# A planned order for the two token halves around each norm, a fourth column behind it, and the layer norm's first mean added in PSUM

## The chip, the cores and the metric

The kernel runs on one core of a Trainium2 chip. Its work is done by TensorE (matrix products, PE in the profile; PEld are its weight loads), VectorE (DVE), ScalarE (ACT) and GpSimd (POOL), and SyncE's queue (SP) starts the transfers. The metric is the device time of one execution in microseconds (us).

## The reference, cut to what matters

The input is a sequence of 512 tokens with 1024 features. A first block of two layers (attention, then a gated spatial unit, each followed by a convolutional feed-forward network) uses RMS norms; a second block of two layers (a recurrent unit, then dilated attention, with two SwiGLU networks each) uses layer norms around scaled residual sums. All is in float32. Around a norm this is computed:

```python
def rms_norm(x, g):
    y = x * rsqrt(mean(x * x, axis=-1, keepdims=True) + EPS)
    return y * g

def layer_norm(x, g, b):
    mu = mean(x, axis=-1, keepdims=True)
    xc = x - mu
    var = mean(xc * xc, axis=-1, keepdims=True)
    return xc * rsqrt(var + LN_EPS) * g + b

x = x + g2 * conv_ffn(modulate(rms_norm(x, ffn_norm[l]), sh2, sc2), ...)
x = layer_norm(DEEPNORM_ALPHA * x + swiglu(x, w_in, w_out), g, b)
```

## The kernel before, in words

Features lie on the partitions: the residual x is eight tiles x0 to x7 of 128 features by 512 tokens. Every product of a weight and an activation is done as three passes of a reduced float32 type, high times high, high times low and low times high (`mm`, lines 190 to 192). A weight chunk (128 output features, up to eight input tiles) is loaded by SyncE's queue and split by `chunk`: ScalarE makes the high part `wh` (line 145), VectorE the low part `wl` (line 148). Three raw and seven split chunks have buffers at a time. Of PSUM's eight banks six (`b1`) serve the products, two (`norm`) the norms.

A stage ends with `out_gemm`: eight output column tiles of 128 features, each a sum over the hidden tiles. `update` adds a finished bank to its x tile (line 468 or 507), ScalarE squares the tile (315), VectorE adds the square to `acc` (316). The last four column tiles (three after the recurrent unit, six before the last norm) are *held*: they are done first for tokens 0 to 255 (half 0), then for 256 to 511 (half 1). So the norm of half 0 can be worked out while TensorE does the held tiles of half 1.

The norm of a half is: column sums of `acc` by TensorE (281); a chain of small VectorE instructions on 128x2 (lines 270 to 274, three Newton steps for the inverse root); a *spread* of the result to rows (copy 287, transposes 291); then eight *rows*, one for each x tile. A row of an RMS norm is one VectorE instruction and a split (ScalarE high, VectorE low). A row of a layer norm is two VectorE instructions (545, 546), the high part (552) and a float32 copy (553) by ScalarE, and the low part by GpSimd (554).

A layer norm also keeps the sum of x in `accs`, by GpSimd (521). To keep the variance exact, the mean over the first 256 features is taken off all tiles as soon as x0 and x1 are done: their sum (510) times a matrix of ones on TensorE (512), scaled by ScalarE (513), is subtracted from x0 to x4 by VectorE and from x5 to x7 by GpSimd (515).

Behind the norm the next stage's `Head` starts its first columns by halves: three columns of a feed-forward network, of the recurrent unit's input, of the keys or of the queries; the spatial unit has its own head over token tiles. Head step k needs row k of the norm. The order within each engine is chosen by the framework's scheduler from its own estimates, from the order of the code and the dependences.

There are ten such norms: four RMS norms (after the first attention, the first convolutional network, the spatial unit and the second network), then six layer norms (after the first SwiGLU network, the recurrent unit, the second network, the third, the second attention and the last network). The last has no head.

## Time and profile before

| what | value |
|---|---|
| median of three runs | 3490.24 us (3489.15 to 3495.66) |
| the profiled execution, and its span | 3490.69 us, 3488.9 us |
| TensorE busy | 3318.5 us, 95% |
| VectorE, ScalarE, GpSimd busy | 59%, 40%, 11% |
| chain that ended last | TensorE 82%, VectorE 10%, ScalarE 3% |
| mean granted clock of TensorE | 0.979 of full speed |

A busy TensorE is one that has an instruction in it; matrix products overlap, so the time of one is read from start to start. The granted clock is 1.00 at the higher of TensorE's two levels and 0.5 at the lower.

### The profile page before, as it was taken

How to read it: one execution, taken by the hardware profiler on the slowest of the kernel's cores; microseconds unless marked ns; L12 is line 12 of the kernel's file. 1: busy time of each engine (PE TensorE's matmuls, PEld its weight loads, DVE VectorE, ACT ScalarE, POOL GpSimd, SP SyncE). 2: the span in 40 equal slices, each digit the busy share in tenths (PEclk: the TensorE clock that was granted, in tenths of full speed). 3: DMA queues.
4: the chain of work that ended last, by engine and by line, in shares of the span. 5: the costliest groups of instructions: out<-in, count | busy, mean ns of one | idle time of the engine just before them, and what ended most of it. 6: DMA issues, size and time to landing. Idle time of an engine off the chain costs nothing.

```text
span 3488.9 us, 43165 instructions
## 1 busy us (share of the span) xinstructions
PE 3318.5 (95%) x16662; PEld 2823.7 (81%) x16662; DVE 2056.9 (59%) x3419; ACT 1403.9 (40%) x2129; POOL 366.9 (11%) x375
## 2 busy tenths in 40 slices
PE   4888899999999999999999999999999899989998
PEld 3777788888888888888888888889888888788887
DVE  8777887865574555333776533363333689873335
ACT  4245643334343333222485422242222466652223
POOL 5043000000000000000313100030000322230001
PEclk9888999999999999999999999999999999999999
DMA  5641355643222322223132323235223133133231
GB/s 187 188 153 43 139 178 196 223 140 102 85 91 97 97 91 91 97 85 104 62 108 77 109 97 97 91 129 186 97 91 98 47 100 101 48 107 105 92 100 46
DMA packets 126207, 381.70 MB, mean 109 GB/s; under 512 B 13745, under 2 KB 28209, under 8 KB 125874
## 3 DMA queue, kind: packets, MB, share of 16 engines
q1 hardware_dynamic: 125858, 378.82, 33.4%
q8 instruction: 131, 2.15, 0.3%
q14 instruction: 74, 0.61, 0.1%
q10 hardware_dynamic: 144, 0.13, 0.0%
HBM read 360.54 MB, written 18.35 MB: 109 GB/s over the span
## 4 chain that ended last, share of the span: by engine, by line
PE 82%; DVE 10%; ACT 3%; issue 2%; DMA 2%; POOL 0%; SPq 0%; DVEq 0%; ACTq 0%; POOLq 0%
PE b L191 24%; PE b L192 24%; PE b L190 24%; PE bo L838 1%; PE side L190 1%; PE side L191 1%; PE side L192 1%; PE b L822 1%; DVE wl L148 1%; DVE x L515 1%; DVE nm L806 1%; DVE ptl L148 1%; DVE acc L316 1%; PE s L730 1%; DVE reg L148 1%
## 5 line engine op out<-in xcount | busy, mean ns | idle before, releaser
L191 PE MATMUL b<-reg,wh 128*128 128x512 f32 (+1 forms) x4289 | 1573.6, 369 | 24.4 <-DVE reg L337 14.9
L190 PE MATMUL b<-reg,wh 128*128 128x512 f32 (+1 forms) x4289 | 1543.3, 369 | 35.8 <-ACT reg L336 12.4
L192 PE MATMUL b<-reg,wl 128*128 128x512 f32 (+1 forms) x4289 | 1568.8, 368 | 2.5 <-DVE wl L148 2.4
L145 ACT ACTIVATE wh<-raw 128x1024 fp32r<-128x1024 f32 (+3 forms) x550 | 561.1, 1026 | 1325.6 <-PE b L191 1170.0
L148 DVE TENSOR_TENSOR wl<-raw,wh 128x1024 fp32r<-128x1024 f32 (+3 forms) x550 | 656.6, 1200 | 563.1 <-ACT wh L145 551.5
L191 PEld LDWEIGHTS b<-reg,wh 128*128 128x128 f32 x4289 | 821.7, 192 | 160.5 <-DVE reg L337 17.5
L190 PEld LDWEIGHTS b<-reg,wh 128*128 128x128 f32 x4289 | 803.3, 191 | 173.8 <-ACT reg L336 14.6
L192 PEld LDWEIGHTS b<-reg,wl 128*128 128x128 f32 x4289 | 820.8, 191 | 134.1 <-DVE wl L148 3.9
L515 POOL TENSOR_TENSOR x<-x,shift 128x512 f32<-128x512 f32 x18 | 30.9, 1741 | 2475.7 <-ACT shift L513 2475.7
L592 DVE TENSOR_TENSOR sg<-sg,b 128x512 f32<-128x512 f32 x88 | 60.5, 688 | 281.9 <-PE b L192 281.2
L1535 DVE SCALAR_TENSOR_TENSOR x<-b,x 128x512 f32<-128x512 f32 x64 | 44.3, 692 | 190.1 <-PE b L192 190.1
L315 ACT ACTIVATE sq<-x 128x256 f32<-128x256 f32 (+1 forms) x111 | 52.6, 474 | 176.8 <-DVE x L507 84.7
L145 ACT ACTIVATE reg<-sg 128x512 fp32r<-128x512 f32 x132 | 83.3, 631 | 79.5 <-DVE sg L597 77.4
L371 DVE CUSTOM_DVE_ANT_0 ada<-ada,silu_c,cols 128x1024 f32<-128x1024 f32 x80 | 99.5, 1281 | 14.4 <-DMA ada<-ada 14.2
L145 ACT ACTIVATE pth<-b 128x384 fp32r<-128x384 f32 (+1 forms) x160 | 82.1, 534 | 63.0 <-PE b L822 60.1
L148 DVE TENSOR_TENSOR ptl<-b,pth 128x384 fp32r<-128x384 f32 (+1 forms) x160 | 94.6, 603 | 19.2 <-ACT pth L145 18.1
L148 DVE TENSOR_TENSOR reg<-sg,reg 128x512 fp32r<-128x512 f32 x132 | 90.6, 686 | 22.3 <-ACT reg L145 22.3
L190 PE MATMUL side<-reg,wh 128*128 128x512 f32 x221 | 98.6, 446 | 4.8 <-DVE hn L651 2.8
L822 PE MATMUL b<-ident,e 128*128 128x128 f32 x544 | 84.1, 283 | 15.0 <-DVE ptl L148 7.8
L822 PEld LDWEIGHTS b<-ident,e 128*128 128x128 f32 x544 | 66.0, 145 | 30.6 <-DVE ptl L148 9.0
L191 PE MATMUL side<-reg,wh 128*128 128x512 f32 x221 | 90.0, 407 | 0.4 <-DVE reg L148 0.4
L192 PE MATMUL side<-reg,wl 128*128 128x512 f32 x221 | 90.0, 407 | 0.0
(331 smaller groups left out, 3586.8 us busy)
## 6 DMA issues: line engine op xcount, KB each, us to landing
raw<-up SPq DMA_DIRECT2D x264, 512.0 KB, 3.3
ada<-ada SPq DMA_DIRECT2D x96, 512.0 KB, 4.6
raw<-down SPq DMA_DIRECT2D x96, 448.0 KB, 3.2
raw<-down SPq DMA_DIRECT2D x48, 512.0 KB, 3.3
raw<-q SPq DMA_DIRECT2D x24, 512.0 KB, 3.5
raw<-rg_in SPq DMA_DIRECT2D x20, 512.0 KB, 3.3
raw<-attn_in SPq DMA_DIRECT2D x14, 512.0 KB, 7.0
raw<-rg_out SPq DMA_DIRECT2D x16, 320.0 KB, 2.9
```

The source lines that it names most:

```text
L145: return self.nc.scalar.activation(out=hi, in_=src, func=AF.Copy, scale=scale)
L148: return self.nc.vector.tensor_tensor(out=lo, in0=src, in1=hi.bitcast(F32), op=ALU.subtract)
L190: mm(out=ps, lhsT=ah, rhs=bh, start=first, stop=False)
L191: mm(out=ps, lhsT=ah, rhs=bl, start=False, stop=False)
L192: mm(out=ps, lhsT=al, rhs=bh, start=False, stop=last)
L315: nc.scalar.activation(out=s, in_=src, func=AF.Square)
L316: nc.vector.tensor_tensor(out=acc, in0=acc, in1=s, op=ALU.add)
L371: self.nc.vector.tensor_tensor_reduce(out=r, in0=r, in1=self.silu_c, scale=1.0, scalar=self.col("ada_b", 48 * l + m), op0=ALU.mult, op1=AL ...
L515: (nc.vector if k < 5 else nc.gpsimd).tensor_tensor(out=self.x[k], in0=self.x[k], in1=self.shift, op=ALU.subtract)
L592: nc.vector.tensor_tensor(out=sg, in0=sg, in1=bu, op=ALU.mult)
L822: nc.tensor.transpose(out=b[:, i * P:(i + 1) * P], in_=e[:, (k0 + i) * P:(k0 + i + 1) * P], identity=self.ident)
L1535: self.nc.vector.scalar_tensor_tensor(out=x[m], in0=b, scalar=c, in1=x[m], op0=ALU.mult, op1=ALU.add)
```

## The change

It has four parts.

- `turn`, a planner: after the held tiles of half 0 it lists the held products of half 1, the updates, the norm chains of both halves, their rows and the head steps with an engine, a rank and a duration written by hand, and emits them in the order in which they would start; TensorE, VectorE, ScalarE and GpSimd then keep the order in which the code is written. Only TensorE and VectorE have a time line in the plan.
- Seven heads (five feed-forward networks, the recurrent unit's input, the keys) start four columns instead of three. The fourth weight chunk is split inside the turn (`more`), since its buffer is that of a held tile.
- A layer norm's first mean is no longer subtracted from x2 to x7. TensorE adds it to the bank of each of those column tiles, with one pass (`shift_pass`) of a constant matrix on the sum of x0 and x1. x0 and x1 get it by VectorE from a bank.
- A square and its sum are issued apart, and a head step does its passes with the high part of the activation for all columns before those with the low part.

```diff
 class Head:
     def begin(self):
-        self.w = [self.net.chunk(*a) for a in self.args]
+        self.w = [self.net.chunk(*a) for a in self.args[:3]]
+        self.out = []
+    def more(self):
+        self.w += [self.net.chunk(*a) for a in self.args[3:]]
...
 class ColumnHead(Head):
+    step = property(lambda self: 0.36 * len(self.args))
...
+            for b, w in zip(self.out, self.w):
+                mm(out=b[:, sl], lhsT=w[0][:, k, :], rhs=h, start=k == 0, stop=False)
+                mm(out=b[:, sl], lhsT=w[1][:, k, :], rhs=h, start=False, stop=False)
+            for b, w in zip(self.out, self.w):
+                mm(out=b[:, sl], lhsT=w[0][:, k, :], rhs=l, start=False, stop=k == KD - 1)
+            yield
...
 def out_gemm(...):
-        for n, sl in enumerate(HALVES):
-            for m, ws in held:
-                b = self.bank()[:, 0:256]
-                one(b, ws, sl)
-                updates()
-                done_banks.append((m, b, sl))
-            updates()
-            if head is not None:
-                if n == 0:
-                    head.begin()
-                else:
-                    head.half(HALVES[0])
-            finish(sl)
+        for m, ws in held:
+            b = self.bank()[:, 0:256]
+            one(m, b, ws, HALVES[0])
+            updates()
+            done_banks.append((m, b, HALVES[0]))
+        updates()
+        head = self.head
         if head is not None:
-            head.half(HALVES[1])
+            head.begin()
+        with self.tc.manual_schedule(engines=FULL_ORDER):
+            self.turn(held, ..., xs, update, [finish(sl) for sl in HALVES], head, shifted)
...
+    def turn(self, held, ks, xs, update, fin, head, shifted):
+        rows_dur = 0.87 if shifted else 0.9
+        chain_dur = 3.7 if shifted else 2.9
+        free = item("wait", 0, 0.0, None)
+        items[free][5] = 1.9
+        sums = [free, None]
...
+                prev = item("PE", 5, 0.36, lambda ...: product(bank, ws, n), () if prev is None else (prev,))
+            x = item("DVE", 0, 0.45, lambda ...: late.append(update(m, bank[0], sl)), (prev,), 0.15)
+            sums[1] = item("DVE", 1, 0.62, lambda late=late: late[0](), (x,), 0.6)
+        more = None if head is None else item("DVE", 3, 1.25, head.more, (free,), 1.3)
+        for n, gen in enumerate(fin):
+            c = item("PE", 1, 0.5 if shifted else 0.25, go(gen), (sums[n],), 0.25 if n else 0.0)
+            c = item("DVE", 2, chain_dur, go(gen), (c,), 0.2)
+            c = item("PE", 0, 0.45 if shifted else 0.25, go(gen), (c,), 0.2)
+            for k in range(KD + 1):
+                c = item("DVE", 4, rows_dur if k < KD else 0.45, go(gen), (c,), 0.0 if k else 0.25)
+                rows.append(c)
+        if head is not None:
+            for n in range(2):
+                gen = head.half(HALVES[n])
+                for k in range(KD):
+                    r = (KD + 1) * n + k
+                    prev = item("PE", 5, head.step, go(gen), (prev,))
+                    items[prev][4] += [(rows[r], 0.7), (rows[r + 1], -rows_dur + 0.02), (more, 0.02)]
...
+                    t = max([at[engine]] + [items[n][5] + lag for n, lag in needs])
+                    if best is None or (t, rank, i) < best[:3]:
...
+        for _, _, f in sorted(plan, key=lambda z: z[:2]):
+            f()
...
+    def shift_pass(self, ps, sl):
+        self.nc.tensor.matmul(out=ps, lhsT=self.mean, rhs=self.shift[:, sl], start=False, stop=True)
...
 def ln_update(self, m, ps, scale, sl):
         if m == 1:
-            s = self.tmp()
-            nc.vector.tensor_tensor(out=s, in0=self.x[0], in1=self.x[1], op=ALU.add)
+            self.mean = self.means[scale]
+            nc.vector.tensor_tensor(out=self.shift, in0=self.x[0], in1=self.x[1], op=ALU.add)
             b = self.bank()
-            nc.tensor.matmul(out=b, lhsT=self.ones, rhs=s, start=True, stop=True)
-            nc.scalar.activation(out=self.shift, in_=b, func=AF.Copy, scale=1.0 / 256)
-            for k in range(KD):
-                (nc.vector if k < 5 else nc.gpsimd).tensor_tensor(out=self.x[k], in0=self.x[k], in1=self.shift, op=ALU.subtract)
+            nc.tensor.matmul(out=b, lhsT=self.mean, rhs=self.shift, start=True, stop=True)
+            for k in range(2):
+                nc.vector.scalar_tensor_tensor(out=self.x[k], in0=b, scalar=scale, in1=self.x[k], op0=ALU.mult, op1=ALU.add)
...
-        return ColumnHead(self, [("up", 44 * i + m, 8) for m in (0, FF, 1)])
+        return ColumnHead(self, [("up", 44 * i + m, 8) for m in FFN_HEAD])
```

What this does to the order of instructions is shown at three places of the first layer norm (after the first SwiGLU network, the fifth of the ten). The first is VectorE while TensorE does the held products of half 1. Before, update 6, the spread's copy, the sums and update 7 come ahead of the first rows (lines 545, 546; `x6` is the x tile, `norm` the spread rows, `sq` a square):

```order
L538 SCALAR_TENSOR_TENSOR ln_y_2487_13489<-ln_s_2488_13490,ln_y_2487_13489 128x2
L507 SCALAR_TENSOR_TENSOR x6_868_3636<-b1_2519_13627,x6_868_3636 128x256
L287 COPY spread_2490_13507<-ln_y_2487_13489 128x512
L316 TENSOR_TENSOR acc_2136_11271<-acc_2136_11271,sq_2522_13677 128x256
L507 SCALAR_TENSOR_TENSOR x7_869_3637<-b1_2521_13654,x7_869_3637 128x256
L545 TENSOR_TENSOR tmp_2508_13530<-x0_862_3630,norm_2491_13509 128x256
L546 TENSOR_TENSOR tmp_2508_13530<-tmp_2508_13530,norm_2491_13509 128x256
L545 TENSOR_TENSOR tmp_2509_13536<-x1_863_3631,norm_2491_13509 128x256
L316 TENSOR_TENSOR acc_2136_11271<-acc_2136_11271,sq_2523_13682 128x256
L546 TENSOR_TENSOR tmp_2509_13536<-tmp_2509_13536,norm_2491_13509 128x256
```

In the changed kernel (651 is the update, 574 the sum, 692 and 693 a row), from the spread's copy on:

```order
L375 COPY spread_2492_13618<-ln_y_2489_13600 128x512
L651 SCALAR_TENSOR_TENSOR x4_866_3634<-b1_2485_13570,x4_866_3634 128x256
L651 SCALAR_TENSOR_TENSOR x5_867_3635<-b1_2493_13620,x5_867_3635 128x256
L163 TENSOR_TENSOR wl_2500_13675<-raw_2498_13672,wh_2499_13674 128x1024
L651 SCALAR_TENSOR_TENSOR x6_868_3636<-b1_2494_13643,x6_868_3636 128x256
L574 TENSOR_TENSOR acc_2142_11390<-acc_2142_11390,sq_2495_13655 128x256
L574 TENSOR_TENSOR acc_2142_11390<-acc_2142_11390,sq_2497_13667 128x256
L574 TENSOR_TENSOR acc_2142_11390<-acc_2142_11390,sq_2502_13691 128x256
L692 TENSOR_TENSOR tmp_2519_13731<-x0_862_3630,norm_2496_13660 128x256
L693 TENSOR_TENSOR tmp_2519_13731<-tmp_2519_13731,norm_2496_13660 128x256
L651 SCALAR_TENSOR_TENSOR x7_869_3637<-b1_2501_13685,x7_869_3637 128x256
```

The low part of the fourth weight chunk (`wl`) now stands between updates 5 and 6, and three sums come behind it, ahead of the first row.

The second place is VectorE at the second chain, that of half 1 (`ln_s`, `ln_v`, `ln_m2`, `ln_y` and `rsq_b` are its 128x2 values). Before, rows of half 0 stand between its instructions:

```order
L546 TENSOR_TENSOR tmp_2511_13548<-tmp_2511_13548,norm_2491_13509 128x256
L545 TENSOR_TENSOR tmp_2512_13554<-x4_866_3634,norm_2491_13509 128x256
L535 TENSOR_TENSOR ln_m2_2529_13767<-ln_s_2531_13769 128x2
L546 TENSOR_TENSOR tmp_2512_13554<-tmp_2512_13554,norm_2491_13509 128x256
L545 TENSOR_TENSOR tmp_2513_13560<-x5_867_3635,norm_2491_13509 128x256
L536 SCALAR_TENSOR_TENSOR ln_v_2528_13766<-ln_m2_2529_13767,ln_v_2528_13766 128x2
L546 TENSOR_TENSOR tmp_2513_13560<-tmp_2513_13560,norm_2491_13509 128x256
L545 TENSOR_TENSOR tmp_2514_13566<-x6_868_3636,norm_2491_13509 128x256
L270 TENSOR_SCALAR ln_y_2530_13768<-ln_v_2528_13766 128x2
L546 TENSOR_TENSOR tmp_2514_13566<-tmp_2514_13566,norm_2491_13509 128x256
L545 TENSOR_TENSOR tmp_2515_13572<-x7_869_3637,norm_2491_13509 128x256
```

In the changed kernel it begins behind row 4 and runs on to its spread's copy without a row between:

```order
L692 TENSOR_TENSOR tmp_2529_13793<-x4_866_3634,norm_2496_13660 128x256
L693 TENSOR_TENSOR tmp_2529_13793<-tmp_2529_13793,norm_2496_13660 128x256
L677 COPY ln_s_2533_13814<-norm_2528_13788 128x2
L678 TENSOR_SCALAR ln_v_2530_13811<-norm_2528_13788 128x2
L679 TENSOR_TENSOR ln_m2_2531_13812<-ln_s_2533_13814 128x2
L680 SCALAR_TENSOR_TENSOR ln_v_2530_13811<-ln_m2_2531_13812,ln_v_2530_13811 128x2
L359 TENSOR_SCALAR ln_y_2532_13813<-ln_v_2530_13811 128x2
L361 TENSOR_TENSOR rsq_b_2534_13819<-ln_y_2532_13813 128x2
L362 SCALAR_TENSOR_TENSOR rsq_b_2534_13819<-rsq_b_2534_13819,ln_v_2530_13811 128x2
L363 SCALAR_TENSOR_TENSOR ln_y_2532_13813<-rsq_b_2534_13819,ln_y_2532_13813 128x2
L361 TENSOR_TENSOR rsq_b_2534_13819<-ln_y_2532_13813 128x2
```

Row 5, which before stood between the chain's instructions, now comes behind the whole chain.

The third place is TensorE at the head's start (`ident`, `spread`: the transposes; `ones`: column sums; `reg0_0` the high part of row 0, `reg0_8` its low part). Before, the spread of half 0 and the column sums of half 1 stand around the first head passes:

```order
L191 MATMUL b1_2521_13654<-reg1_14_2433_13187,wh_2464_13347 128x256
L192 MATMUL b1_2521_13654<-reg1_6_2432_13186,wl_2465_13348 128x256
L291 MATMUL norm_2491_13509<-ident_20_78,spread_2490_13507 128x128 x4
L281 MATMUL norm_2527_13761<-ones_21_80,accs_2137_11272 128x1 x2
L190 MATMUL b1_2524_13686<-reg0_0_2492_13514,wh_2476_13466 128x256
L190 MATMUL b1_2525_13687<-reg0_0_2492_13514,wh_2479_13472 128x256
L190 MATMUL b1_2526_13688<-reg0_0_2492_13514,wh_2482_13478 128x256
L281 MATMUL norm_2527_13761<-ones_21_80,acc_2136_11271 128x1 x2
L191 MATMUL b1_2524_13686<-reg0_8_2500_13522,wh_2476_13466 128x256
L192 MATMUL b1_2524_13686<-reg0_0_2492_13514,wl_2477_13467 128x256
```

In the changed kernel, from the last held product on:

```order
L207 MATMUL b1_2501_13685<-reg1_6_2434_13274,wl_2466_13429 128x256
L645 MATMUL b1_2501_13685<-shift_2144_11392,mean0_2140_11386 128x256
L85 MATMUL b1_2522_13747<-reg0_0_2503_13715,wh_2477_13552 128x256
L86 MATMUL b1_2522_13747<-reg0_0_2503_13715,wl_2478_13553 128x256
L85 MATMUL b1_2523_13748<-reg0_0_2503_13715,wh_2480_13558 128x256
L86 MATMUL b1_2523_13748<-reg0_0_2503_13715,wl_2481_13559 128x256
L85 MATMUL b1_2524_13749<-reg0_0_2503_13715,wh_2483_13564 128x256
L86 MATMUL b1_2524_13749<-reg0_0_2503_13715,wl_2484_13565 128x256
L85 MATMUL b1_2525_13750<-reg0_0_2503_13715,wh_2499_13674 128x256
L86 MATMUL b1_2525_13750<-reg0_0_2503_13715,wl_2500_13675 128x256
L88 MATMUL b1_2522_13747<-reg0_8_2511_13723,wh_2477_13552 128x256
L88 MATMUL b1_2523_13748<-reg0_8_2511_13723,wh_2480_13558 128x256
```

A shift pass (`mean0`) closes the held tile, the spread has moved ahead into the held products, the column sums behind head step 1, and head step 0 has four columns.

## Rows read from the trace of the kernel before

**Rows 1.** Page, busy time by engine, and TensorE's granted clock in forty slices.

```profile
PE 3318.5 (95%) x16662; PEld 2823.7 (81%) x16662; DVE 2056.9 (59%) x3419; ACT 1403.9 (40%) x2129; POOL 366.9 (11%) x375
...
PEclk9888999999999999999999999999999999999999
```

**Rows 2.** Windows: length, busy PE, PEld, DVE, ACT, POOL (instructions), clock, DMA share, GB/s.

```profile
436.00:483.00 47.00, 43.80 (x354) 42.73 (x354) 36.23 (x89) 16.78 (x33) 0.00 (x0) 1.00 0.34 116
802.00:852.00 50.00, 47.60 (x293) 42.29 (x292) 33.64 (x84) 21.69 (x41) 0.00 (x0) 1.00 0.23 73
948.00:997.00 49.00, 47.11 (x370) 45.66 (x369) 31.86 (x82) 17.41 (x32) 0.00 (x0) 1.00 0.15 47
1316.00:1370.00 54.00, 47.68 (x342) 46.18 (x341) 31.07 (x82) 16.64 (x33) 0.00 (x0) 0.91 0.19 61
1690.00:1743.00 53.00, 48.59 (x362) 46.43 (x361) 44.39 (x98) 27.99 (x51) 28.15 (x30) 0.97 0.11 35
1900.00:1953.00 53.00, 50.03 (x375) 48.11 (x375) 44.00 (x93) 29.15 (x52) 26.67 (x28) 0.97 0.15 49
2272.00:2327.00 55.00, 49.87 (x361) 47.71 (x360) 44.36 (x97) 27.23 (x51) 27.93 (x30) 0.94 0.11 35
2735.00:2787.00 52.00, 46.42 (x351) 44.46 (x349) 40.92 (x94) 24.35 (x48) 27.90 (x30) 0.97 0.09 31
3062.00:3126.00 64.00, 56.92 (x393) 53.56 (x392) 52.06 (x104) 34.85 (x58) 29.52 (x30) 0.91 0.26 84
```

**Rows 3.** TensorE's waits, fifth window: total us, times, longest us.

```profile
PE norm L281 <- POOL accs L521: 2.1, 2, 1.2
PE b L191 <- POOL reg L554: 1.0, 2, 0.7
PE b L190 <- ACT reg L552: 1.0, 1, 1.0
```

**Rows 4.** TensorE's waits in the ninth window.

```profile
PE b L190 <- DVE x L507: 2.2, 1, 2.2
```

**Rows 5.** TensorE's time line: start, us, line, operands; eight and fifty starts apart.

```profile
1663.70 0.39 PE L192 MATMUL b<-reg,wl 128*128 128x512 f32 x1
...
1665.52 0.39 PE L191 MATMUL b<-reg,wh 128*128 128x512 f32 x1
...
1709.75 0.28 PE L190 MATMUL b<-reg,wh 128*128 128x256 f32 x1
...
1715.75 0.28 PE L192 MATMUL b<-reg,wl 128*128 128x256 f32 x1
```

**Rows 6.** VectorE by line, fifth window: count, busy us, mean ns, idle before.

```profile
L545 DVE TENSOR_TENSOR tmp<-x,norm 128x256 f32<-128x256 f32 x16 | 6.6, 415 | 0.9 <-PE norm L291 0.9
...
L148 DVE TENSOR_TENSOR wl<-raw,wh 128x1024 fp32r<-128x1024 f32 x5 | 6.4, 1320 | 5.7 <-ACT wh L145 3.5 <-PE b L512 2.2
L316 DVE TENSOR_TENSOR acc<-acc,sq 128x256 f32<-128x256 f32 x8 | 4.7, 585 | 2.5 <-ACT sq L315 2.4
```

**Rows 7.** ScalarE by line, fifth window.

```profile
L552 ACT ACTIVATE reg<-tmp,cols 128x256 fp32r<-128x256 f32 x16 | 9.4, 589 | 4.1 <-DVE tmp L546 4.1
...
L145 ACT ACTIVATE wh<-raw 128x1024 fp32r<-128x1024 f32 x4 | 4.0, 1044 | 0.0
```

**Rows 8.** VectorE's time line: the last norm's second chain, its ends.

```profile
3474.24 0.15 DVE L533 COPY ln_s<-norm 128x2 f32<-128x2 f32 x1
...
3477.25 0.43 DVE L287 COPY spread<-ln_y 128x512 f32<-128x512 f32 x1
```

**Rows 9.** VectorE's time line: the fifth window's second chain.

```profile
1719.41 0.15 DVE L533 COPY ln_s<-norm 128x2 f32<-128x2 f32 x1
...
1724.71 0.59 DVE L273 SCALAR_TENSOR_TENSOR rsq_b<-rsq_b,ln_v 128x2 f32<-128x2 f32 x1
...
1726.88 0.43 DVE L287 COPY spread<-ln_y 128x512 f32<-128x512 f32 x1
```

**Rows 10.** GpSimd's time line, there.

```profile
1724.52 0.77 POOL L554 TENSOR_TENSOR reg<-x,reg 128x256 fp32r<-128x256 f32 x1 [0.24 <-ACT x L553]
```

More of the change, by code (lines that the diff above doesn't have):

```diff
@@ L93, with half @@
 class TokenHead(Head):
-    def products(self, sl, hi, lo):
+    step = 1.36
+    def half(self, sl):
         net = self.net
+        hi, lo = net.h_next
         toks = [slice(t, t + P) for t in range(sl.start, sl.stop, P)]
         banks = [net.bank() for _ in toks]
+        self.out += banks
         for k in range(KD):
@@ L111, in __init__ @@
         self.head = None
+        self.means = {}
     def nm(self, s):
@@ L236, in out_gemm @@
                 b = self.bank()
-                one(b, ws, every)
+                one(m, b, ws, every)
                 updates()
@@ L478, in rms_end @@
     def rms_end(self, sl, a, b):
-        n = sl.stop - sl.start
-        R = self.rms_scale(self.acc[:, sl], n // P, 1024.0, 1e-6)[:, 0:n]
+        nc = self.nc
+        R = yield from self.rms_steps(sl)
         h = self.next_h(sl)
-        for k in range(KD):
-            g = self.affine_split(self.x[k][:, sl], a(k), b(k), h[k][0], h[k][1], R)
-        self.gate = g
+        before = None
+        for k in range(KD + 1):
+            if k < KD:
+                x = self.x[k][:, sl]
+                y = self.tmp()[:, 0:x.shape[1]]
+                nc.vector.scalar_tensor_tensor(out=y, in0=x, scalar=a(k), in1=R, op0=ALU.mult, op1=ALU.mult)
+                g = nc.scalar.activation(out=h[k][0], in_=y, func=AF.Identity, bias=b(k))
+            if before is not None:
+                j, z = before
+                g2 = nc.vector.scalar_tensor_tensor(out=h[j][1], in0=z, scalar=b(j), in1=h[j][0].bitcast(F32), op0=ALU.add,
+                                                    op1=ALU.subtract)
+            before = k, y
+            self.gate = (g, g2) if k else ()
+            yield
@@ L487, in rms_final @@
     def rms_final(self, sl):
[L488 to L489 removed]
+        nc = self.nc
+        R = yield from self.rms_steps(sl)
         h = self.next_h(sl)
[L491 to L495 removed]
@@ L496, in rms_final @@
-        self.gate = g
-    def ln_begin(self):
+        for k in range(KD + 1):
+            if k < KD:
+                x = self.x[k][:, sl]
+                nc.vector.scalar_tensor_tensor(out=x, in0=x, scalar=self.col("final_norm", k), in1=R, op0=ALU.mult, op1=ALU.mult)
+                g = self.hi(h[k][0], x)
+            if k:
+                g2 = self.lo(h[k - 1][1], self.x[k - 1][:, sl], h[k - 1][0])
+                self.gate = g, g2
+            yield
+    def ln_begin(self):
+        self.shifts = True
+        if not self.means:
+            for c in (0.5 / ALPHA, 1.0 / ALPHA):
+                self.means[c] = self.t(self.xp, [P, P], F32R, f"mean{len(self.means)}")
+                self.nc.vector.tensor_scalar(out=self.means[c], in0=self.ident, scalar1=0.0, scalar2=-1.0 / (256.0 * c),
+                                             op0=ALU.mult, op1=ALU.add)
```

156 lines of the change are left out of this document (110 added, 46 removed).

## The prediction

> **What bounds the kernel now.** I read the page first, then the stretches around the norms, what TensorE waited for in them, and last the time lines of VectorE and GpSimd. The page has TensorE busy for 3318.5 of 3488.9 us, and from the fifth of the forty slices on its clock stays at nine tenths or above [rows 1]. So no amount of work taken from VectorE, ScalarE or GpSimd shortens the kernel by itself; only TensorE's own idle time, low clock or work counts. The change touches the ten norms. The table of windows shows what they lose [rows 2]. Idle time is the window's length less TensorE's busy time. The low clock costs the window's length times what the granted clock lacks of 1.00 (at the lower level, 1.2 of 2.4 GHz, a stretch loses half its length).
>
> The four RMS stretches lie idle 3.20, 2.40, 1.89 and 6.32 us, together 13.8, and the fourth, at 0.91, loses 0.09 x 54 = 4.9 to the clock: 18.7 us. The five layer norms that feed a head lie idle 4.41, 2.97, 5.13, 5.58 and 7.08 us, together 25.2; at 0.97, 0.97, 0.94, 0.97 and 0.91 the clock costs 1.6, 1.6, 3.3, 1.6 and 5.8 us: 39.1 us. So 57.8 us are to be had at most, 1.7% of the kernel. The tenth norm has no head, so its end is a plain chain that the change does not shorten.
>
> What TensorE waits for in the first layer-norm stretch is GpSimd's running sum of x (2.1 us in two waits), the low part of a head operand, which GpSimd makes (1.0), and its high part, from ScalarE (1.0) [rows 3]. At the last one a product also waits 2.2 us for a bank, because the update that empties it stands behind the subtractions of the mean on VectorE [rows 4].
>
> **The change part by part.** *Work added to TensorE.* A product 128x512 takes (1665.52 - 1663.70) / 8 = 0.227 us from start to start, one of 256 columns (1715.75 - 1709.75) / 50 = 0.120 [rows 5]. A layer norm with a head gets two passes of 512 and eight of 256 (after the recurrent block three and six), 1.4 us each, the last norm twelve of 256, 1.4 too: 6 x 1.4 = 8.5. The product with the ones, once in each, is replaced by one with fewer instructions; that is worth between nothing and one 0.227 each, and I take the latter, so 7.1 us are left. Seven heads do their fourth column in halves: 24 x (2 x 0.120 - 0.227) = 0.31 us each, 2.2. Together 9.3 us on the path: TensorE is the bound, nothing hides them.
>
> *Work taken from VectorE and GpSimd.* The 30 and 18 subtractions are off the path except at the bank wait of 2.2 us at the ninth norm, and, in part, where they delay the first running sums. I value them at that wait. They could be worth up to the 2.1 us of running-sum waits in each layer norm; both ends are in the range.
>
> *The order in an RMS norm.* The four RMS windows show GpSimd at 0.00 [rows 2], so rows and chain run at VectorE's own pace. A head step of four columns is 12 x 0.120 = 1.44 us, longer than a row of two VectorE instructions of some 0.42 [rows 6], so once it has started TensorE finds its operand ready. What is left is the head's start. The half-1 products last 4 x 24 x 0.120 = 11.5 us. In that time VectorE does a chain, four updates, a weight cast and four late sums. It comes out level, and I leave 0.3, 0.5, 0.3 and 0.9 us: 2.0 of 18.7, so 16.7 are won. If the cast is not covered it is 1.65 us more each time (below).
>
> *The order in a layer norm.* I laid the new order of the first one (after the first SwiGLU block) against durations of before, from the end of the half-0 products at 0. An update and a square (I take 0.42 for each, as for a row's instruction), the late sum (0.59) [rows 6], the column sums and the handovers let the chain start at 2.9. Alone it takes 3477.25 + 0.43 - 3474.24 = 3.4 us with the spread [rows 8]: 6.3. Two updates: 7.1. Now VectorE reaches the cast of the fourth column's weights. ScalarE's half of it (1.04 [rows 7]) is queued behind the squares of these two updates, so VectorE stands still until 8.75 and casts until about 10 (1.32 [rows 6]). Then come an update, three late sums (0.59) and row 0 with two instructions (0.42): 12.5. ScalarE adds 0.59 [rows 7] and a handover: the first high part is there at 13.15, while the half-1 products, 4 x 21 x 0.120 and four shift passes, column sums and spread, end at 11.5. So TensorE waits 1.65, and some 0.45 more for the first low part, a GpSimd instruction later.
>
> The second chain now stands in one piece between rows 4 and 5 (before, the rows of half 0 went on between its instructions). In the trace a two-input VectorE instruction of 128x2 that meets GpSimd's low part takes 0.59, where the copy that starts the chain takes 0.15, and ends when GpSimd does: 1724.71 + 0.59 against 1724.52 + 0.77 [rows 9, 10]. Two low parts are still due when the chain starts, so I give it 3.4 + 2 x 0.45 = 4.3 us. The head has work for about 4.3 us then, but the spread and row 5 are needed next: TensorE waits 0.7, 0.9 and 0.4 us. Sum: 4.1 us idle, and, as before the change, one low-clock stretch worth 1.6. So 5.7 where the first window lost 4.41 + 1.6 = 6.0.
>
> The Trainium skill (page "SBUF — State Buffer", section "Who interferes with whom") says that a VectorE instruction with two SBUF inputs contends with a GpSimd instruction that reads SBUF, and the loser waits for the whole instruction. The 0.59 us row agrees. Its rule speaks against putting twelve such instructions in one piece; without it the chain would be 0.9 us shorter and the sum some 5 us lower.
>
> The others by the same working: 5.5 after the recurrent block (three held tiles; two of the head's weight casts now stand around the first chain), 5.7 before keys and values, 5.7 + 1.6 = 7.3 before the second attention (three columns, so no cast, but a head step of only 9 x 0.120 = 1.08 us covers less of the chain: one more low-clock stretch), 5.7 + 2 x 1.32 = 8.3 at the ninth, where two weight casts [rows 6] stand among the last updates and hold up the column sums. Together 5.7 + 5.5 + 5.7 + 7.3 + 8.3 = 32.5 of 39.1: 6.6 won.
>
> *Sum.* 16.7 + 6.6 - 9.3 = 14.0 us less. The profiled execution took 3490.69 us (0.45 above the median of the three runs, so the difference carries over): 3476.2 from the median, 3476.7 from the profiled one. I say 3476.5. About 7 us, 0.2%, is what a measurement of this kernel can tell from no change.
>
> **The rivals.**
> - *The order does what it is written for.* Cast and second chain are hidden, layer norms keep about 1 us each, and the clock holds. For it: in the three RMS windows without a loss of clock, gaps up to 3.2 us cost nothing more. Against it: the standstill before the cast is in the order itself. 39.1 - 6.1 = 33 won there, 33 + 16.7 - 9.3 = 40: 3450.
> - *Gains are given back.* The cast holds up the three RMS heads too, 3 x 1.65 = 5.0, and each of the five layer norms falls to the lower clock once more, 5 x 1.6 = 8.0 (for it: the third and fifth of them show two such stretches or more at similar idle times). 14.0 - 13.0: 3489, no change.
> - *Slower: the second chain in one piece.* If GpSimd's low parts meet nearly every two-input instruction of it, the chain lasts as long as before the change, 1726.88 + 0.43 - 1719.41 = 7.9 us [rows 9], but with no row served in it. 3 us and more of further waiting and one more low-clock stretch of 1.6, in five norms: 23 us, so 3490 + 9 = 3499. It decides from a chain of about 5.5 us on: 5 x (1.2 + 1.6) = 14. Against it: GpSimd has only two or three low parts due at that point.
> - *The subtraction's move does not pay.* If VectorE was not what delayed the bank at the ninth norm, 2.2 us come back, 3479. This lies inside the forecast's own range.
>
> **How the numbers follow.** The forecast has a chance of 0.50 with a range of its own of 3466 to 3486; full recovery 0.17, no change 0.18, slower 0.15. The bounds of the unknown terms (running sums 0 to 2.1 us in five norms, chain 3.4 to 7.9, cast hidden or not) span 3450 to 3499. Cutting what is beyond 8 in 10 gives 3449 to 3495. Faster by over 0.2% (below 3483.3): 0.17, most of the forecast's 0.50 and a little of the third case, 0.65. Within 0.2%: 0.19. Slower (above 3497.2): 0.16.
>
> **What would show it.** In the profile after: RMS windows with under 1 us idle each and a clock of 1.00, the fourth above all (right step), or waits on ScalarE's high part of 1.6 us at the head's start (cast not covered). In the layer norms the wait on the high part at the head's start, a second pair of waits on spread and row 5, and second-chain instructions stretched to 0.5 us or more; their absence means the first rival, a block over 5.5 us the third. No bank wait at the ninth norm. TensorE's instructions up by 229. If the windows outside the norms change by more than 2 us in sum, the forecast rests on the wrong places.

## The result, and the profile after

The changed kernel takes 3456.07 us (median of four runs, 3454.42 to 3456.71) against 3492.47 us of the kernel before in the same comparison: a ratio of 0.9895, 95% interval 0.9878 to 0.9912, so 36.4 us less. The forecast was 14.0 less. The direction and the range held, the size did not: the time lies nearer to the first rival, 40 us less, than to the forecast. The profiled execution took 3456.31 us with a span of 3454.5, 34.4 less than that of before [rows 1 for its busy time].

The page of the changed kernel, busy time by engine:

```profile
PE 3304.6 (96%) x16885; PEld 2823.4 (82%) x16885; DVE 2027.9 (59%) x3403; ACT 1399.6 (41%) x2122; POOL 334.0 (10%) x357
```

TensorE issues 223 more matrix instructions in this trace (229 were forecast) and is busy 13.9 us less. At the nine norms of the windows the low clock costs 3.5 us now, where it cost 18.8 (4.9 + 13.9). The windows of the changed kernel that answer to [rows 2], same columns (length, busy times with counts, clock, DMA share, GB/s):

```profile
435.40:482.90 47.50, 47.50 (x398) 47.45 (x398) 36.98 (x88) 17.77 (x32) 0.00 (x0) 1.00 0.41 145
801.10:846.00 44.90, 44.21 (x278) 39.39 (x278) 31.76 (x80) 20.69 (x39) 0.00 (x0) 1.00 0.18 56
943.70:991.10 47.40, 47.40 (x398) 47.38 (x397) 31.02 (x79) 16.80 (x31) 0.00 (x0) 1.00 0.18 58
1309.30:1354.70 45.40, 44.81 (x374) 44.57 (x373) 30.01 (x79) 15.63 (x31) 0.00 (x0) 1.00 0.20 66
1673.40:1724.10 50.70, 48.53 (x395) 47.17 (x394) 36.56 (x89) 25.19 (x48) 21.47 (x26) 1.00 0.12 37
1881.70:1932.80 51.10, 49.79 (x405) 48.45 (x404) 37.06 (x87) 28.19 (x49) 20.04 (x24) 1.00 0.19 62
2251.40:2302.30 50.90, 48.69 (x395) 47.29 (x395) 36.59 (x89) 25.39 (x48) 21.51 (x26) 1.00 0.13 41
2709.60:2758.00 48.40, 43.04 (x346) 41.36 (x344) 33.64 (x88) 22.85 (x46) 21.50 (x26) 1.00 0.10 34
3035.90:3094.90 59.00, 54.29 (x421) 53.03 (x421) 44.94 (x99) 31.32 (x55) 24.23 (x27) 0.94 0.27 84
```

Idle time, read as before: 0, 0.69, 0 and 0.59 us in the RMS norms, and the clock at 1.00 in all four. In the layer norms it is 2.17, 1.31, 2.21, 5.36 and 4.71 us, and only the ninth lost to the clock, 0.06 x 59 = 3.5. (Of the 5.36 some 1.4 us stand at the window's end, at the next stage's first product; of the 5.58 before, some 1.2.) So the RMS norms keep 1.3 us of 18.7, the layer norms 19.3 of 39.1. 17.4 and 19.8 are won, and 37.2 - 34.4 leaves 2.8 us for the added work and everything outside the windows.

TensorE's waits in the fifth and in the ninth window:

```profile
PE b L85 <- ACT reg L699: 2.0, 2, 1.3
...
PE norm L370 <- POOL accs L662: 3.9, 1, 3.9
PE b L85 <- ACT reg L699: 0.7, 1, 0.7
```

The running-sum wait of [rows 3] is gone from the fifth window, as is the wait on GpSimd's low part; what is left is ScalarE's high part, twice. At the ninth the bank wait of [rows 4] is gone and a wait of 3.9 us for the first column sums has come.

VectorE's time line at the first layer norm: the cast in the turn, and the second chain's first and last instructions with the two that are stretched:

```profile
1692.85 1.23 DVE L163 TENSOR_TENSOR wl<-raw,wh 128x1024 fp32r<-128x1024 f32 x1 [1.49 <-ACT wh L160]
...
1702.08 0.16 DVE L677 COPY ln_s<-norm 128x2 f32<-128x2 f32 x1 [0.56 <-PE norm L370]
...
1702.27 0.63 DVE L679 TENSOR_TENSOR ln_m<-ln_s 128x2 f32<-128x2 f32 x1
...
1703.13 0.76 DVE L359 TENSOR_SCALAR ln_y<-ln_v 128x2 int32<-128x2 int32 x1
...
1705.88 0.43 DVE L375 COPY spread<-ln_y 128x512 f32<-128x512 f32 x1
```

GpSimd's low parts beside that chain:

```profile
1702.14 0.75 POOL L701 TENSOR_TENSOR reg<-x,reg 128x256 fp32r<-128x256 f32 x1 [0.25 <-ACT x L700]
1703.12 0.74 POOL L701 TENSOR_TENSOR reg<-x,reg 128x256 fp32r<-128x256 f32 x1 [0.24 <-ACT x L700]
```

TensorE there: the last held product, the head's start with its wait, the second column sums, the end of head step 4, the spread, and head step 5 with its wait:

```profile
1696.07 0.28 PE L645 MATMUL b<-shift,mean 128*128 128x256 f32 x1
1697.62 0.39 PE L85 MATMUL b<-reg,wh 128*128 128x256 f32 x1 [1.26 <-ACT reg L699]
1697.84 0.28 PE L86 MATMUL b<-reg,wl 128*128 128x256 f32 x1
...
1701.09 0.50 PE L370 MATMUL norm<-ones,accs 128*128 128x1 f32 x4
1701.45 0.59 PE L370 MATMUL norm<-ones,acc 128*128 128x1 f32 x4
...
1705.81 0.64 PE L88 MATMUL b<-reg,wh 128*128 128x256 f32 x4
1706.46 0.63 PE L382 MATMUL norm<-ident,spread 128*128 128x128 f32 x4
1707.78 0.39 PE L85 MATMUL b<-reg,wh 128*128 128x256 f32 x1 [0.70 <-ACT reg L699]
```

VectorE stands still for 1.49 us before the cast, as the replay had it (1.65). The chain takes 1705.88 + 0.43 - 1702.08 = 4.2 us (4.3), stretched by two low parts (0.63 and 0.76 us). But TensorE comes to the spread without a wait, and has one single wait of 0.70 us after it, where the replay had 0.7, 0.9 and 0.4.

### The profile page after: what moved, and what is told of

Its sections match the earlier page's. It is cut to its first block, busy times and chain, and to the rows that moved or that the text cites. A ratio compares the mean times of both kernels' runs of the same rounds, so it can differ in the third digit from the quotient of the medians.

```text
span 3454.5 us, 43538 instructions
## 1 busy us (share of the span) xinstructions
PE 3304.6 (96%) x16885; PEld 2823.4 (82%) x16885; DVE 2027.9 (59%) x3403; ACT 1399.6 (41%) x2122; POOL 334.0 (10%) x357
## 4 chain that ended last, share of the span: by engine, by line
PE 82%; DVE 8%; ACT 4%; issue 4%; DMA 1%; POOL 1%; SPq 0%; ACTq 0%; POOLq 0%; DVEq 0%
PE b L206 23%; PE b L205 23%; PE b L207 23%; PE b L88 1%; PE side L205 1%; PE b L85 1%; PE bo L985 1%; PE b L86 1%; PE side L206 1%; PE side L207 1%; PE b L969 1%; DVE wl L163 1%; DVE ptl L163 1%; DVE nm L953 1%; ACT wh L160 1%
## 5 line engine op out<-in xcount | busy, mean ns | idle before, releaser
L205 PE MATMUL b<-reg,wh 128*128 128x512 f32 (+1 forms) x3849 | 1440.0, 375 | 21.5 <-ACT reg L430 9.5
L206 PE MATMUL b<-reg,wh 128*128 128x512 f32 (+1 forms) x3849 | 1441.0, 375 | 15.2 <-DVE reg L431 12.9
L207 PE MATMUL b<-reg,wl 128*128 128x512 f32 (+1 forms) x3849 | 1438.7, 374 | 2.9 <-DVE wl L163 2.9
L205 PEld LDWEIGHTS b<-reg,wh 128*128 128x128 f32 x3849 | 728.9, 189 | 153.2 <-ACT reg L430 11.0
L206 PEld LDWEIGHTS b<-reg,wh 128*128 128x128 f32 x3849 | 729.2, 189 | 144.7 <-DVE reg L431 14.6
L207 PEld LDWEIGHTS b<-reg,wl 128*128 128x128 f32 x3849 | 728.8, 189 | 131.7 <-DVE wl L163 4.1
L660 POOL TENSOR_TENSOR accs<-x,x 128x512 f32<-128x512 f32 x6 | 10.2, 1708 | 2452.3 <-DVE x L658 2452.3
L85 PE MATMUL b<-reg,wh 128*128 128x256 f32 x496 | 126.3, 287 | 7.1 <-ACT reg L699 6.5
L86 PE MATMUL b<-reg,wl 128*128 128x256 f32 x496 | 124.3, 283 | 0.0
L465 DVE CUSTOM_DVE_ANT_0 ada<-ada,silu_c,cols 128x1024 f32<-128x1024 f32 x80 | 99.5, 1280 | 13.2 <-DMA ada<-ada 13.1
L163 DVE TENSOR_TENSOR ptl<-b,pth 128x384 fp32r<-128x384 f32 (+1 forms) x160 | 94.4, 603 | 17.7 <-ACT pth L160 16.4
L205 PE MATMUL side<-reg,wh 128*128 128x512 f32 x221 | 98.4, 445 | 4.7 <-DVE hn L798 2.7
L85 PEld LDWEIGHTS b<-reg,wh 128*128 128x128 f32 x496 | 94.9, 191 | 9.1 <-ACT reg L699 8.2
```

The source lines that it names most:

```text
L85: mm(out=b[:, sl], lhsT=w[0][:, k, :], rhs=h, start=k == 0, stop=False)
L86: mm(out=b[:, sl], lhsT=w[1][:, k, :], rhs=h, start=False, stop=False)
L163: return self.nc.vector.tensor_tensor(out=lo, in0=src, in1=hi.bitcast(F32), op=ALU.subtract)
L205: mm(out=ps, lhsT=ah, rhs=bh, start=first, stop=False)
L206: mm(out=ps, lhsT=ah, rhs=bl, start=False, stop=False)
L207: mm(out=ps, lhsT=al, rhs=bh, start=False, stop=last)
```

## The experiments

All times are medians, each beside runs of the kernel before on the same chip. There were three batches on three chips, in which the kernel before took 3492.2 to 3492.9. The first five runs take the change apart.

Some differences are read from start to start: from a norm's first product of 256 columns to that of another norm, compared with the kernel before. This leaves out what comes ahead of the first norm. There the changed kernel and all runs made from it that have the new mean execute the same instructions in the same order, and yet the last product of 512 columns ahead of the first norm starts anywhere from 432.05 us (both orders) to 436.71 us (both orders with three columns):

```profile
432.05 0.39 PE L207 MATMUL b<-reg,wl 128*128 128x512 f32 x1
```

```profile
436.71 0.39 PE L207 MATMUL b<-reg,wl 128*128 128x512 f32 x1
```

So a few us between two single executions say nothing of the change until it is seen in which stretch they lie.

**The fourth column away.**

```diff
-FFN_HEAD = (0, FF, 1, FF + 1)
+FFN_HEAD = (0, FF, 1)
...
-cols("rg_in", (RNN, RNN + 1, 0, 1)) ... cols("kv_k", range(4))
+cols("rg_in", (RNN, RNN + 1, 0)) ... cols("kv_k", range(3))
-more = None if head is None else item("DVE", 3, 1.25, head.more, (free,), 1.3)
+more = None if head is None or len(head.args) < 4 else item(...)
```

> The changed kernel with three head columns instead of four in the seven column heads, and no weight cast inside the turn. The kernel before took 3492.5 us, the changed one 3456. Theory A (the written order is what pays; the fourth column is only cover): about 3464, since a head step of 1.08 us covers the second chain less, some 1 to 1.5 us more idle in each layer norm, and 2.2 us less work of half columns. Rival B (the fourth column is what covers the waits, the order needs it): above 3475, with low-clock stretches back in at least three of the five layer-norm windows. Rival C (the cast in the turn is the worst wait): faster than 3456, no wait at the head's start.

3454.54 us, ratio 0.9889 (0.9875 to 0.9904): the changed kernel's time to within the spread of the runs. Theories A and B missed; of rival C the mechanism is there, but no gain that stands clear of the spread. The first layer norm's waits:

```profile
PE norm L382 <- DVE spread L375: 1.2, 1, 1.2
PE b L85 <- ACT reg L699: 0.7, 1, 0.7
```

Without the cast the head starts on time (no 1.3 us), without the longer steps the second chain is not covered (the spread, 1.2 us, and row 5). One replaces the other.

**The old mean in the new order.**

```diff
-nc.tensor.matmul(out=b, lhsT=self.mean, rhs=self.shift, start=True, stop=True)
-for k in range(2):
-    nc.vector.scalar_tensor_tensor(out=self.x[k], in0=b, scalar=scale, in1=self.x[k], ...)
+nc.tensor.matmul(out=b, lhsT=self.ones, rhs=s, start=True, stop=True)
+nc.scalar.activation(out=self.shift, in_=b, func=AF.Copy, scale=1.0 / 256)
+for k in range(KD):
+    (nc.vector if k < 5 else nc.gpsimd).tensor_tensor(out=self.x[k], in0=self.x[k], in1=self.shift, op=ALU.subtract)
```

> The changed kernel with the first mean subtracted on VectorE and GpSimd as before; order and four columns stay. Theory A: about 3456 plus or minus 5, the 61 shift passes (some 5 to 8 us of work) go and about as much waiting comes back ahead of the turn, at the ninth norm above all. Rival D (the subtractions taken from VectorE and GpSimd are what keeps the layer norms supplied): above 3470, with the running-sum wait of 2 us back in each layer norm and a low clock in at least three.

3478.55 us, ratio 0.9958 (0.9944 to 0.9973): 22.5 above the changed kernel. Theory A's 5 us are out, rival D is borne out. The first layer norm:

```profile
PE norm L370 <- POOL accs L657: 2.8, 1, 2.8
```

The running sums on GpSimd, behind its three subtractions, are late for the column sums, which the held order puts 1.9 us into the half-1 products: 2.8 us. The same wait stands in the third and the fourth layer norm.

**The mean in PSUM alone**, in the code and order of before.

```diff
-nc.scalar.activation(out=self.shift, in_=b, func=AF.Copy, scale=1.0 / 256)
-for k in range(KD): ... subtract(x[k], x[k], self.shift)
+for k in range(2): x[k] = b * scale + x[k]
...
+if shifted and m > 1:
+    self.shift_pass(b, sl)
 update(m, b, sl)
```

> The kernel before with only the mean added in PSUM; scheduler's order, three columns. Theory A: 3490 to 3497, the shift passes cost 5 to 8 us, the bank wait of 2.2 us at the ninth norm goes and part of the 2.1 us running-sum waits. Rival D: below 3480.

3485.99 us, ratio 0.9981 (0.9972 to 0.9991): 7 less, between the two. The first layer norm:

```profile
PE norm L286 <- POOL accs L536: 1.7, 1, 1.7
PE b L191 <- ACT reg L567: 1.7, 1, 1.7
```

One of the two running-sum waits of [rows 3] goes, but the other lasts 1.7 us, and the head's wait on ScalarE grows from 1.0 to 1.7.

**The fourth column alone**, in the order of before.

```diff
-ColumnHead(self, [("up", 44 * i + m, 8) for m in (0, FF, 1)])
+ColumnHead(self, [("up", 44 * i + m, 8) for m in (0, FF, 1)], [("up", 44 * i + FF + 1, 8)])
```

> The kernel before with only a fourth head column, the scheduler's order. Theory A: 3485 to 3495, the scheduler leaves the chains between the rows and the waits where they were. Rival B: below 3478, since longer head steps cover the second half's waits whatever the order.

3507.79 us, ratio 1.0041 (1.0027 to 1.0055): 15 us slower, beyond both. VectorE and then TensorE at the first RMS norm's second chain:

```profile
472.18 0.16 DVE L306 TENSOR_SCALAR rms_v<-norm 128x2 f32<-128x2 f32 x1 [7.04 <-PE norm L281]
```

```profile
PE norm L291 <- DVE spread L287: 2.6, 1, 2.6
```

VectorE is idle for 7.0 us until the second column sums come, which stand deeper among the longer head's passes in TensorE's queue, and TensorE then waits 2.6 us for the spread, as it did not before. From start to start this norm's stretch is 4.3 us longer than before, that of the third RMS norm 5.5.

**The order alone**: three columns and the old mean, the two edits to the changed kernel above together.

```diff
-FFN_HEAD = (0, FF, 1, FF + 1)
+FFN_HEAD = (0, FF, 1)
...
-        self.shifts = True
+        self.shifts, self.ln = False, True
```

> The changed kernel with three head columns and the mean subtracted on VectorE and GpSimd as before: the written order alone. From the runs so far: the four RMS stretches should keep their 18 us, the layer norms lose what the run with the old mean lost. Theory E (the order and the mean in PSUM pay only together in the layer norms, since the written order puts the column sums where the running sums on GpSimd are ready only without the subtractions): 3475 to 3482, with the running-sum wait near 2.8 us in the layer norms. Rival F (the loss of that run came from four columns together with the old mean): below 3468.

3479.87 us, ratio 0.9966 (0.9953 to 0.9979): theory E. The first layer norm waits for the running sums as with four columns:

```profile
PE norm L370 <- POOL accs L657: 2.8, 1, 2.8
```

So with the old mean the order is worth 12.6 us, with the new one 3485.99 - 3454.54 = 31.5; the mean in PSUM 6.9 us in the old code, 25.3 in the new order; the fourth column costs 15 in the old code and nothing that can be told in the new.

**Longer waits.** To see whether the clock term of the forecast was wrong in itself:

```diff
+if k == 0 and sl.start == 0 and not last:
+    for _ in range(5):
+        nc.vector.tensor_tensor(out=x, in0=x, in1=x, op=ALU.max)
```

> The changed kernel with five more VectorE instructions of 128x256 (x0 = max(x0, x0), 0.42 us each, 2.1 us together) ahead of the first row of half 0 in the five layer norms that feed a head; what is computed stays the same. They put the idle time of a window near the 4.1 us that the forecast had. Theory G (the forecast's rule was right that such waits bring a low-clock stretch, only the waits were smaller): idle time up by about 2 us in each of the five, and a low-clock stretch in at least three of the four windows that had none: 3456 + 10 + 3 x 1.7 = 3471 or more. Rival H (the clock holds at 4 us of idle time in a window if it is in two or three pieces): 3462 to 3467, no low clock but at the ninth norm.

3473.26 us (3464.64 to 3473.59), ratio 0.9937 (0.9921 to 0.9954): theory G in three of the four executions, the profiled one among them; the fourth, 3464.64, lies where rival H has it. The windows of the first four layer norms:

```profile
1673.00:1728.00 55.00, 51.05 (x402) 49.85 (x401) 39.08 (x96) 26.78 (x50) 21.45 (x26) 0.97 0.14 46
1885.00:1936.00 51.00, 46.83 (x370) 45.57 (x369) 35.65 (x89) 24.21 (x45) 19.65 (x24) 0.97 0.16 53
2258.90:2311.00 52.10, 48.29 (x383) 47.25 (x382) 37.80 (x94) 25.09 (x47) 21.50 (x26) 0.97 0.10 33
2719.70:2773.00 53.30, 44.42 (x347) 42.91 (x345) 37.23 (x96) 24.95 (x50) 21.49 (x26) 0.95 0.09 31
```

Each is back below 1.00. The first one's waits:

```profile
PE b L85 <- ACT reg L702: 3.9, 2, 3.6
```

One wait of 3.6 us stands nearly alone there, and 0.03 x 55 = 1.6 us is lost to the clock. The five stretches have 9.7 us more of idle time; the rest of the 17 is left for the clock. That such a stretch needs so long a wait does not follow; the run with both orders (below) has them behind shorter ones.

**The order left to the scheduler.**

```diff
-with self.tc.manual_schedule(engines=FULL_ORDER):
+with ExitStack():
```

> The changed kernel's code in the planned order, but with the framework's scheduler free to order it. Theory A (the order has to be held): above 3470, the scheduler puts rows between the instructions of the chains again. Rival I (the order of the code, the split sums and the new head steps suffice): below 3460.

3457.81 us, ratio 0.9901 (0.9886 to 0.9915): within 2 us of the changed kernel, rival I. But the parts differ. The fourth RMS norm of this run:

```profile
PE norm L370 <- DVE acc L574: 1.5, 1, 1.5
PE b L85 <- ACT reg L160: 1.2, 1, 1.2
```

In the RMS norms the held order is better: from the start of the first norm to that of the fifth the changed kernel wins 18.7 us, this one 8.6. From the fifth to the last the changed kernel wins 14.9, this one 22.8: at the third layer norm, for one, its waits sum to 1.5 us against 2.2.

**A later first column sum at the ninth norm.**

```diff
-items[free][5] = 1.9
+items[free][5] = 5.0      # at the ninth norm alone
```

> The changed kernel with one number of the plan changed at the ninth norm: the first column sums are planned 5.0 us into the half-1 products instead of 1.9. Theory J (TensorE's wait of 3.9 us there is the plan's, since the running sums are late behind two weight casts): the wait goes, and the low-clock stretch with it: 3456 - 3.9 - 3.4 = 3449. Rival K (the wait moves to the head's start, as the chain starts no earlier): 3454 to 3457.

3455.24 us (3451.47 to 3456.59), ratio 0.9893 (0.9876 to 0.9909): not told from the changed kernel. In the profiled execution, the fastest of the four, the ninth norm's stretch is 2.9 us shorter and keeps the clock, but part of the wait moved to the head's start, as rival K has it:

```profile
PE b L85 <- ACT reg L699: 3.0, 2, 2.4
PE norm L370 <- POOL accs L662: 1.0, 1, 1.0
```

**Both orders**: held in the RMS norms, the scheduler's in the layer norms.

```diff
-with self.tc.manual_schedule(engines=FULL_ORDER):
+with ExitStack() if shifted else self.tc.manual_schedule(engines=FULL_ORDER):
```

> The changed kernel with the planned order held in the four RMS norms and the framework's scheduler free in the six layer norms. By the stretches of the runs so far the held order won 18.7 us in the RMS norms against 8.6 of the scheduler's, and 14.9 in the five layer norms with a head against 22.8. Theory N (the two parts add): 3456 - 8 = 3448 to 3450. Rival O (the layer norms of the free run gain from what the scheduler did ahead of them): 3454 or more.

3451.87 us (3451.02 to 3452.64), ratio 0.9887 (0.9872 to 0.9901). This is the fastest version that was run; its slowest run is faster than the fastest of the changed kernel, though the intervals of the two ratios overlap. It falls short of theory N by 2 to 4 us, and the traces do not put even this gain into the norms. Of the 4.3 us between its profiled execution and the changed kernel's, 3.1 lie ahead of the first norm, where the instructions are the same. From start to start the RMS norms win 18.7 us, as with the held order, but the layer norms 16.4: 1.5 more than the changed kernel's 14.9, and not the 22.8 of the scheduler's run. The first and the third layer norm:

```profile
1672.00:1722.00 50.00, 48.54 (x385) 47.59 (x384) 35.66 (x89) 24.80 (x47) 20.58 (x26) 0.97 0.11 35
2249.70:2300.00 50.30, 48.78 (x399) 47.82 (x398) 37.39 (x90) 26.27 (x50) 21.36 (x26) 1.00 0.12 38
```

TensorE's waits in the first and then in the third:

```profile
PE norm L370 <- POOL accs L662: 1.0, 1, 1.0
PE b L85 <- ACT reg L699: 0.4, 1, 0.4
```

```profile
PE norm L370 <- POOL accs L662: 0.9, 1, 0.9
PE b L85 <- ACT reg L699: 0.4, 1, 0.4
```

The waits are the same, and short; the clock is 0.97 in the one and 1.00 in the other. The second and the fourth layer norm have such a stretch too (0.97 and 0.96), where the scheduler's run and the changed kernel have none. So part of what separates these runs is which waits happened to be followed by the lower clock.

**The cast ahead of the updates.**

```diff
-more = None if head is None else item("DVE", 3, 1.25, head.more, (free,), 1.3)
+more = None if head is None else item("DVE", -1, 1.25, head.more, (free,), 1.3)
```

> The changed kernel with the rank of the fourth weight cast in the plan lowered, so that it stands right behind the first chain, ahead of the half-1 updates, and ScalarE's part ahead of their squares. Theory P (TensorE's wait of 1.3 us at the head's start in the first and third layer norm comes from VectorE standing still for ScalarE's part of the cast): these waits go, 3452 to 3454. Rival Q (the updates and the late sums come later by the cast and the wait moves to the second column sums or the second spread): 3456 or more.

3454.11 us (3450.61 to 3455.54), ratio 0.9891 (0.9873 to 0.9909): inside what theory P says, but not told from the changed kernel, and its waits did not go. The first layer norm:

```profile
PE b L85 <- ACT reg L699: 1.8, 2, 1.1
```

VectorE there:

```profile
1690.28 1.22 DVE L163 TENSOR_TENSOR wl<-raw,wh 128x1024 fp32r<-128x1024 f32 x1
...
1693.45 0.42 DVE L651 SCALAR_TENSOR_TENSOR x<-b,x 128x256 f32<-128x256 f32 x1 [1.28 <-PE b L645]
1693.79 1.83 DVE L574 TENSOR_TENSOR acc<-acc,sq 128x256 f32<-128x256 f32 x3
1695.53 0.41 DVE L692 TENSOR_TENSOR tmp<-x,norm 128x256 f32<-128x256 f32 x1
```

The wait at the head's start is 1.1 instead of 1.3. The cast finds its input ready, and VectorE stands still at update 6 instead, 1.28 us, for TensorE's product. So the standstill before the cast was not what sets the head's start: update 6, three late sums and row 0 behind them are, and the plan puts them in that order.

**Both orders with the old mean.**

```diff
-with self.tc.manual_schedule(engines=FULL_ORDER):
+with ExitStack() if finish is not None and self.ln else self.tc.manual_schedule(engines=FULL_ORDER):
...
-        self.shifts = True
+        self.shifts, self.ln = False, True
```

> As the kernel with the held order in the RMS norms and the scheduler's in the layer norms, with the mean subtracted on VectorE and GpSimd as before. Theory R (in the layer norms the mean in PSUM is what pays, whoever sets the order, because the subtractions delay the running sums): 15 us or more above that kernel, 3463 or more, with the running-sum wait of 2 us and more in each layer norm. Rival S (the order of the code and the split sums pay): within 6 us of it.

3463.14 us, ratio 0.9919 (0.9904 to 0.9935): 11.3 above the one it is compared with, between R's 15 and S's 6. The running sums are late twice in the first layer norm, as before the change:

```profile
PE norm L370 <- POOL accs L657: 2.1, 2, 1.2
```

Of the 11.7 us between the two profiled executions 3.3 lie ahead of the first norm and 8.9 in the five layer-norm stretches. So the mean in PSUM is worth some 9 to 11 us where the scheduler orders the layer norms, and 22 to 25 in the held order, which cannot give way when the sums are late.

**Both orders with three columns.**

```diff
-with self.tc.manual_schedule(engines=FULL_ORDER):
+with ExitStack() if shifted else self.tc.manual_schedule(engines=FULL_ORDER):
...
-FFN_HEAD = (0, FF, 1, FF + 1)
+FFN_HEAD = (0, FF, 1)
```

> As the kernel with the held order in the RMS norms and the scheduler's in the layer norms, with three head columns. Theory T (the fourth column buys nothing: its half columns and its cast cost what its cover saves): 3447 to 3452. Rival U (with the scheduler's order the fourth column is the cover for the second chain): 3456 or more.

3458.08 us (3454.40 to 3460.61), ratio 0.9904 (0.9888 to 0.9920): 6 us slower, in rival U's range. Of the 8.6 us between the two profiled executions, though, 4.7 lie ahead of the first norm; 0.4 lie in the RMS norms and 3.6 in the layer norms. So in the scheduler's order the fourth column is cover, worth some 4 us in these traces. With three, the head of the first layer norm is through with half 0 before row 0 of half 1 is there, and waits 1.2 us for its high part:

```profile
PE b L85 <- ACT reg L699: 1.2, 1, 1.2
```

## Why the prediction was right or wrong

- **The RMS norms were right.** 16.7 us forecast, 17.4 measured by the windows, and the run without the mean in PSUM keeps them: with the old mean the same four stretches are shorter by 18.3 us from start to start. With three columns they are shorter by 18.3 too, so the longer head step that I named is not needed for it.
- **The step that failed is the layer norm's term**, "5.7 where the first window lost 6.0" and its sum, 6.6 us won of 39.1. 19.8 were won. Of the 20.4 us between the forecast's 14.0 and the 34.4 of the profiled executions this term makes 13.2; the added work and everything outside the windows make 6.5, the RMS norms 0.7. The mechanisms in it were there (the standstill, the stretched chain, the wait at the head's start), their sizes were not. The five were to keep 22.9 us of idle time and 9.6 of clock; they keep 15.8 and 3.5. In the first one the waits were 1.26 and 0.70 us with some 0.2 in pieces, not 4.1. The column sums of half 1 hold TensorE from 1701.09 until 1702.04; the three head steps behind them lasted until 1706.45, and the chain was through at 1706.31, so the spread's 0.7 was no wait. Row 5's two waits of 0.9 and 0.4 were one of 0.70. The replay's sum was wrong besides: from 10, the update, the three sums and row 0 with the durations that it names end at 13.0 and not at 12.5, so its 1.65 at the head's start should have been 2.2.
- **The clock term** was 9.6 us and came to 3.5. I added a low-clock stretch to each layer norm as if the waits of before were still there. In the changed kernel's execution none came in the first four, with waits of at most 1.3 us. In the padded one, with waits of 2.7 to 3.6 us, one came in each of the four. But that none came is in part luck: the run with both orders has stretches in three of the five layer norms, behind waits no longer than these. The "gaps up to 3.2 us" that I held against the clock term were a sum of four waits of at most 1.1 us.
- **"I value them at that wait"**: the subtractions were priced at 2.2 us. Put back into the held order they cost 22.5. My replay had let the first column sums start on time, so their gain was inside the order's term, and I did not see that the order rests on them: with them in place that order makes the five layer-norm stretches 8.5 us slower than before the change, from start to start. That the step was priced from the waits of the old order was the error.
- **The added work** was to cost 9.3 us; 2.8 us are left for it and all else. The start of the kernel, ahead of the first norm, is 1.3 us shorter, and the recurrent stage has one low-clock stretch less (1.7). So the windows outside changed by more than the 2 us that I had named as a sign against the forecast, but both are within chance: between runs that execute the same instructions there the start varies by 4.7 us, and the recurrent stage by one such stretch. For the other 3.5 us the windows are a poor measure. A wait costs more than its idle time: from the product at 1696.07 to the one at 1697.84 1.77 us pass, where two steps of 0.12 would take 0.24. That is 1.53 us for a wait that shows as 1.26, or 0.27 more. In the nine windows the waits of over 0.05 us fell from 42 to 23; 19 x 0.27 = 5 us is an estimate from these rows, and enough to cover the rest.
- **The ninth norm** was right in size, 8.3 us forecast and 4.71 + 3.5 = 8.2 measured, but in part by luck: 6.7 of the 8.3 were idle time and 1.6 the clock. The bank wait went and a wait for the column sums came. The cast of the weights ahead of them and the running sums are both late there; which of the two sets it was not taken apart (GpSimd's last sum ends at 3055.03, VectorE's at 3055.31, and the column sums begin at 3055.09).
- **The rivals.** Full recovery (3450) was nearest, partly by luck: it had 33 us won in the layer norms, where 19.8 were, and the full cost of the added work; and the standstill that spoke against it is there. The third rival's long chain did not come: GpSimd had two low parts due, and the chain took 4.2 us. And that holding the order paid in the layer norms is not shown: with the same code the scheduler's order won 16.4 and 22.8 us there, the held one 14.9, and 16.7 and 17.5 in the two runs that change one number of its plan.

## What to carry to other kernels

A fixed order rests on when its inputs are ready; work taken from engines that are off the critical path can be worth ten times its visible wait once an order is built on it, and where it was taken back that order lost in the layer norms. So price parts of such a change together, or replay the new order both with and without each part. A clock term belongs to the waits that are left, not to the waits of before, and one execution does not settle it. A hand-written order is worth holding only where it beats the scheduler: here it did in the four RMS norms, and in the layer norms no run shows that it does. And before a few us between two kernels are put down to a change, look whether they lie where the change is.

## What the runs showed of the hardware

- A window's granted clock did not follow from its waits alone. With a wait of 2.7 to 3.6 us it was 0.95 to 0.97 in the four windows of the padded run, with waits of 1.3 and 0.7 us it was 1.00 in the changed kernel. But in the run with both orders two windows with the same waits, about 1.0 and 0.4 us, had 0.97 and 1.00.
- A VectorE instruction with one tensor input, the integer step of the inverse root (128x2), was stretched too beside GpSimd: 0.76 us at 1703.13, ending with the low part that began at 1703.12 and took 0.74. The stretched ones that I had looked at before had two. The Trainium skill (page "SBUF — State Buffer", section "Who interferes with whom") lists such an instruction too, when it runs in a two-port mode; no run here shows the mode.
